# Buffers, a shared key transpose, crossbar-free memory tiles and a reordered start-up in a hybrid encoder layer on one core

## The chip, the cores and the metric

The kernel runs on one core of a Trainium2 chip. A core has a matrix engine (TensorE, PE in the profile; its weight loads are the rows PEld), a vector engine (VectorE, DVE), an activation engine (ScalarE, ACT), GpSimd (POOL) and SyncE (SP), which in this kernel issues every DMA; the rows SPq are its queue. The metric is the device time of one execution in microseconds; less is better. The kernel before takes 3039.52 us, the median of three runs (3033.03 to 3044.13).

## The reference

One encoder layer is applied to two sequences of 4096 and 1024 rows of width 1024 with shared weights. In short:

```python
h = rms_norm(x, norm_in)
z = h @ w_in                          # (L, 1024) @ (1024, 3584)
z_hy, z_att, z_mq, gate = split(z)    # 1152 | 1152 | 256 | 1024 columns
# Hyena branch: centred 3-tap convolution per channel, then an FFT-length convolution
x0, x1, v = split(short_conv3(z_hy));  s = x1 * v
y_hy = x0 * (irfft(rfft(s, 2L) * rfft(filter(L), 2L))[:L] + s * skip)
# 6 heads of 64, three strided windows (128,1) (512,4) (2048,16), merged by their softmax denominators
q, k = head_rms(q), head_rms(k)
y_att = merge(softmax(q k^T / 8 + bias[rel * dil] within |rel| <= R) v  for each window)
# 4 heads of 64 over 256 memory rows
y_mem = softmax(head_rms(z_mq) km^T / 8) vm
out = x + (concat(y_hy, y_att, y_mem) * silu(gate)) @ w_out
```

The filter of the Hyena branch is a small sine network over the positions times an exponential decay per channel.

## The kernel before

**Precision.** The large products are made of three 16-bit matmuls: a value is split into a high and a low fp16 part, and PE adds hi*hi, hi*lo and lo*hi in PSUM (`mm3`, lines 279 to 281). One product of a 128-column weight block with 512 rows is 8 x 3 = 24 matmuls. PSUM has eight banks, given out by tags: "d" has two, "e" two, "f" three and "g" one.

**Stages.** The trace shows five. (1) Start-up: rows of the first block of x are loaded and normed, the first Hyena weight blocks are loaded (`ws`), scaled by the norm gain on POOL (L248), measured on DVE and split by ACT and DVE (L260, L262) into `wh`. (2) `hyena_proj`: ten blocks of 512 rows by nine 128-channel products, tile `zh`; ACT copies each product from PSUM to `zb` (L877), and ACT and DVE apply the three taps (L887, L891). Between them runs the filter stream: `f` (L710), its decay `kt` (L715), a first transform `a` (L732) whose result goes to `fav` (L736, L737). (3) `qkv` products (`z`) woven with the long convolution. (4) Attention woven with the gate products (`zg`). (5) The output product (`oo`).

**One attention tile.** 128 queries of one window, or of the memory. Scores `s` are made by PE from `kT` and `qT`, and from `qS` for half of the heads (L1044, L1047; for the memory L1039). DVE adds the bias and takes the maximum (L1051), negates it (`nm`, L1061), and ACT exponentiates (L1063). The probabilities `pt` must then be transposed and split into fp16 halves. For the first XT = 2 heads of each tile POOL splits them (`hl`, L1079 and L1080) and a transposing DMA, the crossbar, turns them into `hx` (L1082). For the other heads PE transposes in fp32 (`tt`, L1094, four 128x128 blocks for a pair of heads), ACT makes the high half `th` (L1098) and DVE the low half `tl` (L1099). PE multiplies by v (`yp`, L1118 to L1120), ACT, POOL and DVE write the result to `y` (L1155, L1156), and SP stores it to DRAM (`yc`, or `ym` for memory tiles).

**Loads of a group.** Two tiles that share 256 queries form a group; a group's loads are written two groups ahead (AHEAD). `load_group` (L926) asks for three things: the keys `kT` by a transposing DMA of up to 384 rows (L945), the queries `qT` (L946; L933 for memory groups), and `v`. Then DVE makes `qS` (L969), `qT` with the two halves of its partitions exchanged, since a matmul takes both operands from the same partitions.

**What sets the order.** Each stream is a Python generator that yields the cost of what it has just written; `weave` takes the next step from the stream with the least cost so far:

```python
    while live:
        s = min(live, key=lambda v: v[1])
        tc.cur_priority = s[2]
        try:
            s[1] += next(s[0])
```

PE keeps that written order (`manual_schedule` on PE). On every other engine, SP among them, the framework's scheduler orders the instructions by a simulated time line and the priorities; at run time each engine executes its list in order and waits where an operand or a buffer isn't ready. K_A scales the cost of the attention stream against the gates.

Of the kernel before, what the change touches and what calls it, by code (L numbers as in the profile page):

```python
# [22 lines left out]
P = 128  # L23
# [116 lines left out]
K_A, IDLE_A, GATE_IDLE = 0.88, 20000, 0  # L140
LAG_I, WS_BUFS = 6, 6
MT, BATCH0 = 4, 2
MIX, K_Q = 0.1, 1.2
AHEAD = 2
# [34 lines left out]
class Layer:  # L179
# [105 lines left out]
    def setup(self):  # L285
# [9 lines left out]
        self.cinv = {}  # L295
        for i, (off, L) in enumerate(self.seqs):
# [18 lines left out]
    def setup_late(self):  # L315
        nc, c, x = self.nc, self.const, self.x
        self.g_mem = c.tile([P, KC], F32, name="g_mem")
        self.ld(self.g_mem, x["mem_norm"][0].rearrange("(k p) -> p k", p=P))
        self.S_v = c.tile([P, H], F32, name="S_v")
        self.S_mem = c.tile([P, 4], F32, name="S_mem")  # L320
        gains = c.tile([P, 4, E], F32, name="gains")
# [4 lines left out]
        a = c.tile([P, 2, 4], F32, name="gsc")  # L326
# [13 lines left out]
        self.dft = c.tile([P, 4, P], F16, name="dft")  # L340
        self.ld(self.dft, x["dft"].rearrange("p (a b) -> p a b", a=4))
        for i in range(len(self.seqs)):
            self.cinv[i] = c.tile([P, 2, 64], F16, name=f"cinv{i}")
            self.ld(self.cinv[i], x[f"cinv{i}"].rearrange("p (a b) -> p a b", a=2))
# [158 lines left out]
    def memory_weights(self, pool, wpool):  # L503
        nc, x = self.nc, self.x
        self.wm = wm = pool.tile([P, KC, 2, 512], F16, name="wm", bufs=1)
        S = self.S_mem
        for j in (0, 2):
            self.wsplit(
                wpool, self.wparts(x["w_mem_kv"][0], [(j + d, (j + d) * P) for d in range(2)], wm), S[:, j:j + 2],
                self.g_mem, tag="wms", bufs=2,  # L510
            )
# [56 lines left out]
    def bias_tables(self, pool, ps):  # L568
        nc, x, c = self.nc, self.x, self.const
        oh = pool.tile([32, 3, 3 * P], F32, name="oh", bufs=1)  # L570
# [55 lines left out]
    def filter_time(self, pool, psf, small, w1, w2, w3s, delta, m):  # L626
        nc, x = self.nc, self.x
        hid, dec, step, ksum = {}, {}, {}, {}
        for i, (off, L) in enumerate(self.seqs):
# [3 lines left out]
            dec[i] = pool.tile([P, DH], F32, name=f"dec{i}", bufs=1)  # L633
# [70 lines left out]
        def taps(n):  # L704
# [11 lines left out]
            nc.gpsimd.tensor_tensor(out=dec[i], in0=dec[i], in1=step[i], op=ALU.mult)  # L716
# [114 lines left out]
    def hyena_proj(self, pool, ps):  # L831
# [18 lines left out]
        wh, cw, cb = self.hy  # L850
        self.tc.cur_priority += 1500000
        for n, (i, b) in enumerate(blocks):
# [11 lines left out]
            for c in range(3):  # L864
                us = []
                for g in range(3):
# [3 lines left out]
                    z = ps.tile([P, 512], F32, tag="d", name="zh", bufs=2)  # L870
# [35 lines left out]
    def att_tiles(self):  # L906

        out = []
        for i, (off, L) in enumerate(self.seqs):
            for cf, (win, dil) in enumerate(CONFIGS):  # L910
# [6 lines left out]
                for r in range(dil):  # L917
                    for q0 in range(0, n, 256):
                        q1 = min(n, q0 + 256)
                        out.append(dict(  # L920
# [69 lines left out]
    def attention(self, pool, ps):  # L990
# [8 lines left out]
        for g in groups[1:AHEAD]:  # L999
            self.load_group(pool, g)  # L1000
# [682 lines left out]
```

## Time and profile before

| | before |
|---|---|
| median of three runs | 3039.52 us (3033.03 to 3044.13) |
| the profiled execution | 3053.22 us, span 3051.3 us |
| PE busy | 2787.6 us (91%) |
| DVE, ACT, POOL busy | 2054.2, 1663.9, 1263.1 us |
| main DMA queue (SP) | 761578 packets, 75.5% of 16 engines' span |

Busy times are unions of the intervals in which an engine executes. A row of a "waits" view names the instruction that stood first in its engine's list, the instruction whose end released it, the idle time in total, how often, and the longest. A time line's row gives in square brackets the idle time just before it. A "chain" row gives start, length and the link of the chain of work that ended last. In the windows, PEclk is the granted clock of TensorE as a share of its full 2.4 GHz: 0.5 is the lower level of 1.2 GHz. For a DMA row of SPq the duration is that of issuing, not of the transfer.

### The profile page before, as it was taken

The numbers are of one execution on the slowest core, as the hardware profiler recorded it, in microseconds if no ns is written. First come the engines' busy times: TensorE is split into PE (matmuls) and PEld (weight loads), VectorE is DVE, ScalarE is ACT, GpSimd is POOL, SyncE is SP. The second block draws the span as 40 slices with busy tenths as digits, with TensorE's granted clock in tenths as the row PEclk, the third lists the DMA queues.
The fourth block names the chain that finished last, engine by engine and source line by source line (L and its number), as shares of the span: only waits on it lengthen the run. The fifth ranks groups of instructions, "written<-read, shape, count | busy, mean of one in ns | idle before, by whom it ended". The sixth has DMA issues, their size and how long they took to land.

```text
span 3051.3 us, 55381 instructions
## 1 busy us (share of the span) xinstructions
PE 2787.6 (91%) x19620; PEld 1730.6 (57%) x19620; DVE 2054.2 (67%) x5237; ACT 1663.9 (55%) x3149; POOL 1263.1 (41%) x1534
## 2 busy tenths in 40 slices
PE   5898888888899998989999988989899899999999
PEld 2344444334455545544466666666666665778787
DVE  7777888779758872464477666767676666665663
ACT  5666666434668875474266555656566564233321
POOL 3336777343126651151133233333344344555551
PEclk9999999999999999999999999999999999999999
DMA  8555444565579969778499988999998979777762
GB/s 223 176 135 162 133 145 150 170 182 180 195 228 249 249 189 216 220 185 189 134 214 242 218 206 177 219 217 185 209 221 195 206 169 316 247 240 253 236 225 97
DMA packets 761855, 610.38 MB, mean 200 GB/s; under 512 B 514958, under 2 KB 702262, under 8 KB 758122
## 3 DMA queue, kind: packets, MB, share of 16 engines
q1 hardware_dynamic: 761578, 606.84, 75.5%
q8 instruction: 155, 2.54, 0.4%
q14 instruction: 122, 1.00, 0.1%
HBM read 289.08 MB, written 199.92 MB: 160 GB/s over the span
## 4 chain that ended last, share of the span: by engine, by line
PE 37%; DVE 16%; DMA 16%; ACT 7%; issue 6%; POOL 4%; SPq 2%; DVEq 0%; ACTq 0%; POOLq 0%
DMA qT<-rows 5%; PE zg L279 3%; PE zg L280 3%; PE z L279 3%; PE z L280 3%; PE zg L281 3%; PE z L281 3%; PE tt L1094 3%; PE oo L281 2%; PE oo L279 2%; PE oo L280 2%; PE s L1044 2%; DMA gg<-gt 1%; DVE qS L969 1%; PE s L1047 1%
## 5 line engine op out<-in xcount | busy, mean ns | idle before, releaser
L1063 ACT ACTIVATE pt<-pt,nm 128x256 f32<-128x256 f32 (+2 forms) x880 | 350.0, 472 | 187.6 <-DVE nm L1061 178.3
L279 PE MATMUL z<-wA,hA 128*128 128x512 f16 (+1 forms) x960 | 353.9, 369 | 19.8 <-ACT rw L440 11.2
L280 PE MATMUL z<-wA,hA 128*128 128x512 f16 (+1 forms) x960 | 353.2, 368 | 0.0
L281 PE MATMUL z<-wA,hA 128*128 128x512 f16 (+1 forms) x960 | 353.0, 368 | 0.0
L1051 DVE CUSTOM_DVE_ANT_0 pt<-s,tab,lsc 128x256 f32<-128x256 f32 (+1 forms) x672 | 278.6, 449 | 98.6 <-PE s L1047 91.2
L279 PE MATMUL zh<-hB,wh 128*128 128x512 f16 x720 | 280.6, 390 | 27.1 <-ACT zb L877 26.8
L280 PE MATMUL zh<-hB,wh 128*128 128x512 f16 x720 | 280.2, 389 | 1.5 <-DVE hB L384 1.5
L281 PE MATMUL zh<-hB,wh 128*128 128x512 f16 x720 | 279.9, 389 | 0.0
L279 PE MATMUL oo<-wo,mhi 128*128 128x512 f32 x640 | 258.5, 404 | 7.1 <-ACT mhi L1537 3.9
L281 PE MATMUL oo<-wo,mlo 128*128 128x512 f32 x640 | 254.8, 398 | 1.6 <-POOL mlo L1538 1.6
L280 PE MATMUL oo<-wo,mhi 128*128 128x512 f32 x640 | 254.6, 398 | 0.0
L1079 POOL CAST hl<-pt 128x256 f16<-128x256 f32 (+1 forms) x212 | 102.8, 499 | 356.5 <-ACT pt L1063 274.3
L279 PE MATMUL zg<-hG,wg 128*128 128x512 f16 x640 | 247.7, 387 | 0.6 <-DVE vr L475 0.5
L281 PE MATMUL zg<-hG,wg 128*128 128x512 f16 x640 | 247.2, 386 | 0.0
L280 PE MATMUL zg<-hG,wg 128*128 128x512 f16 x640 | 247.2, 386 | 0.0
L1099 DVE TENSOR_TENSOR tl<-tt,th 128x512 f16<-128x512 f32 (+1 forms) x280 | 187.8, 673 | 64.6 <-ACT th L1098 62.7
L1098 ACT ACTIVATE th<-tt 128x512 f16<-128x512 f32 (+1 forms) x280 | 159.3, 574 | 107.6 <-PE yp L1120 54.5
L1094 PE MATMUL tt<-ident,pt 128*128 128x128 f32 x1088 | 172.8, 281 | 40.7 <-DVE tl L1099 29.3
L1044 PE MATMUL s<-kT,qT 128*128 128x256 f16 (+2 forms) x720 | 167.4, 263 | 41.6 <-DVE mx L1051 36.4
L1080 POOL TENSOR_TENSOR hl<-pt,hl 128x256 f16<-128x256 f32 (+1 forms) x212 | 192.0, 913 | 6.4
L891 DVE SCALAR_TENSOR_TENSOR u<-zb,cw,u 128x512 f32<-128x512 f32 (+2 forms) x180 | 163.9, 914 | 36.0 <-ACT u L887 32.7
L1094 PEld LDWEIGHTS tt<-ident,pt 128*128 128x128 f32 x1088 | 131.2, 144 | 76.3 <-issue 36.7
(303 smaller groups left out, 7194.1 us busy)
## 6 DMA issues: line engine op xcount, KB each, us to landing
y<-yc SPq DMA_DIRECT2D x120, 198.0 KB, 4.7
yc<-y SPq DMA_DIRECT2D x112, 198.0 KB, 3.2
xt<-in_x SPq DMA_DIRECT2D x40, 512.0 KB, 4.7
hts<-hB SPq DMA_DIRECT2D x10, 2048.0 KB, 6.5
hA<-hts SPq DMA_DIRECT2D x40, 512.0 KB, 6.3
rows<-rw SPq DMA_DIRECT2D x40, 512.0 KB, 4.1
hG<-hts SPq DMA_DIRECT2D x10, 2048.0 KB
gt<-go SPq DMA_DIRECT2D x80, 256.0 KB, 3.3
```

The costliest lines, as they stand in the source:

```text
L279: nc.tensor.matmul(out, pick_l(lh, k), pick_r(rh, k), start=(k == 0), stop=False)
L280: nc.tensor.matmul(out, pick_l(lh, k), pick_r(rl, k), start=False, stop=False)
L281: nc.tensor.matmul(out, pick_l(ll, k), pick_r(rh, k), start=False, stop=(k == n - 1))
L891: nc.vector.scalar_tensor_tensor(out=u[:, :w], in0=zb[:, c0 + d:c1 + d], scalar=cw[:, j, tap:tap + 1], in1=u[:, :w], op0=ALU.mult, op1=ALU ...
L1044: nc.tensor.matmul(s[:, a, :W], g["qT"][:, h, qs], g["kT"][:, h, kc:kc + W], start=True, stop=False,)
L1051: nc.vector.tensor_tensor_reduce(out=pt[:, h, :W], in0=s[:, a, :W], in1=zero.to_broadcast([P, NMEM]) if mem else tb[:, h, t0:t0 + W], scal ...
L1063: nc.scalar.activation(out=pt[:, h, :W], in_=pt[:, h, :W], func=AF.Exp, bias=nm[:, h:h + 1])
L1079: nc.gpsimd.tensor_copy(hl[:, 0, :, c], src)
L1080: nc.gpsimd.tensor_tensor(out=hl[:, 1, :, c], in0=src, in1=hl[:, 0, :, c], op=ALU.subtract)
L1094: nc.tensor.transpose(tt[:, a, ci, :], pt[:, 2 * pr + a, w0:w0 + P], self.ident)
L1098: nc.scalar.activation(out=th[:, :, :n], in_=tt[:, :, :n], func=AF.Copy)
L1099: nc.vector.tensor_tensor(out=tl[:, :, :n], in0=tt[:, :, :n], in1=th[:, :, :n], op=ALU.subtract)
```

## The change

The diff has these parts:

1. `hyena_proj`: the PSUM tile of `zh` rotates over tags "d", "g", "d", so three banks instead of two; "g" has no other user in that stage.
2. Start-up: BATCH0 2 to 4 puts the first block's four row tiles into one norm chain; WS_BUFS 6 to 3 leaves three buffers for raw Hyena weights; of `setup_late`, the load of the transform `dft` stays there, the gains `gk`, `lsc` move into `bias_tables`, the load of `g_mem` into `memory_weights`, that of `cinv` into `long_conv`.
3. Filter: the decay `dec` gets a second buffer, and its last update is left out.
4. Keys: one `kT` transpose of up to 640 rows serves two groups (KG = 512), with three buffers as before; the `qT` transpose is issued first.
5. `qS`: its two copies move from `load_group` to `swap_queries`, which is written at the last tile of the group before.
6. Memory tiles: XT = 0 for them, so all their heads are transposed on PE.
7. Buffers in attention: `th` and `tl` 4 to 6, `y` 2 to 3; the bias tables are loaded one by one into two buffers.
8. K_A 0.88 to 0.84.

```diff
--- before.py
+++ after.py
...
-K_A, IDLE_A, GATE_IDLE = 0.88, 20000, 0
-LAG_I, WS_BUFS = 6, 6
-MT, BATCH0 = 4, 2
+K_A, IDLE_A, GATE_IDLE = 0.84, 20000, 0
+LAG_I, WS_BUFS = 6, 3
+MT, BATCH0 = 4, 4
 MIX, K_Q = 0.1, 1.2
-AHEAD = 2
+AHEAD, KG = 2, 512
...
-    def setup_late(self):
+    def setup_transforms(self):
+        self.dft = self.const.tile([P, 4, P], F16, name="dft")
+        self.ld(self.dft, self.x["dft"].rearrange("p (a b) -> p a b", a=4))
+
+    def setup_gains(self, pool):
+
         nc, c, x = self.nc, self.const, self.x
-        self.g_mem = c.tile([P, KC], F32, name="g_mem")
-        self.ld(self.g_mem, x["mem_norm"][0].rearrange("(k p) -> p k", p=P))
-        self.S_v = c.tile([P, H], F32, name="S_v")
-        self.S_mem = c.tile([P, 4], F32, name="S_mem")
-        gains = c.tile([P, 4, E], F32, name="gains")
+        gains = pool.tile([P, 4, E], F32, name="gains")
         for i, nm in enumerate(("att_q_norm", "att_k_norm", "mem_q_norm", "mem_k_norm")):
             self.ld(gains[:, i], x[nm][0].partition_broadcast(P))
         self.gk = c.tile([P, 2, E], F32, name="gk")
         nc.vector.tensor_tensor(out=self.gk, in0=gains[:, 0:4:2], in1=gains[:, 1:4:2], op=ALU.mult)
-        a = c.tile([P, 2, 4], F32, name="gsc")
+        a = pool.tile([P, 2, 4], F32, name="gsc")
...
-        self.dft = c.tile([P, 4, P], F16, name="dft")
-        self.ld(self.dft, x["dft"].rearrange("p (a b) -> p a b", a=4))
-        for i in range(len(self.seqs)):
-            self.cinv[i] = c.tile([P, 2, 64], F16, name=f"cinv{i}")
-            self.ld(self.cinv[i], x[f"cinv{i}"].rearrange("p (a b) -> p a b", a=2))
...
+        self.setup_gains(pool)
...
-            dec[i] = pool.tile([P, DH], F32, name=f"dec{i}", bufs=1)
+            dec[i] = pool.tile([P, DH], F32, tag=f"dec{min(i, 1)}", name="dec", bufs=2 - min(i, 1))
...
-            nc.gpsimd.tensor_tensor(out=dec[i], in0=dec[i], in1=step[i], op=ALU.mult)
+            d = dec[i]
+            if n2 + 1 < 2 * self.seqs[i][1] // N1:
+                dec[i] = pool.tile([P, DH], F32, tag="dec0", name="dec", bufs=2)
+                nc.gpsimd.tensor_tensor(out=dec[i], in0=d, in1=step[i], op=ALU.mult)
...
+                    nz += 1
-                    z = ps.tile([P, 512], F32, tag="d", name="zh", bufs=2)
+                    z = ps.tile([P, 512], F32, tag="dgd"[nz % 3], name="zh", bufs=2 - nz % 3 % 2)
...
-                    for q0 in range(0, n, 256):
-                        q1 = min(n, q0 + 256)
-                        out.append(dict(
-                            seq=i, cf=cf, dil=dil, r=r, n=n, pair=False, q0=q0, nq=q1 - q0,
-                            k0=max(0, q0 - 64), k1=min(n, q1 + 64),
-                        ))
+                    for b0 in range(0, n, KG):
+                        b1 = min(n, b0 + KG)
+                        keys = dict(b0=b0, k0=max(0, b0 - 64), k1=min(n, b1 + 64))
+                        for q0 in range(b0, b1, 256):
+                            q1 = min(n, q0 + 256)
+                            out.append(dict(
+                                seq=i, cf=cf, dil=dil, r=r, n=n, pair=False, q0=q0, nq=q1 - q0, keys=keys,
+                                k0=max(0, q0 - 64), k1=min(n, q1 + 64),
+                            ))
...
-        kT = pool.tile([P, 6, 384], F16, tag="kT", name="kT", bufs=AHEAD + 1)
-        nk = g["k1"] - g["k0"]
+        if g["cf"] not in self.tab:
+            self.load_table(pool, g["cf"])
+        if g["pair"] or g["q0"] == g["keys"]["b0"]:
+            kT = pool.tile([P, 6, KG + P], F16, tag="kT", name="kT", bufs=3)
...
-            nc.sync.dma_start_transpose(out=kT[:, :, :nk], in_=rows[r, g["k0"]:g["k1"], C_K:ROW])
             nc.sync.dma_start_transpose(
                 out=qT[:, :, :g["nq"]], in_=rows[r, g["q0"]:g["q0"] + g["nq"], C_Q:C_MQ]
             )
+            keys = g["keys"]
+            if g["q0"] == keys["b0"]:
+                keys["kT"] = kT
+                nc.sync.dma_start_transpose(
+                    out=kT[:, :, :keys["k1"] - keys["k0"]], in_=rows[r, keys["k0"]:keys["k1"], C_K:ROW]
+                )
+            kT = keys["kT"]
             cuts = [g["k0"]] + list(range(g["q0"] + 64, g["k1"], 128))
...
+    def swap_queries(self, pool, g):
+
+        if "mem" in g:
+            return
+        nc, qT = self.nc, g["qT"]
         qS = g["qS"] = pool.tile([P, 6, 256], F16, tag="qS", name="qS", bufs=2)
         for a in range(2):
             nc.vector.tensor_copy(
@@ -994,10 +1017,10 @@
...
-        self.load_group(pool, groups[0])
-        self.load_tables(pool)
-        for g in groups[1:AHEAD]:
+        self.tab = {}
+        for g in groups[:AHEAD]:
             self.load_group(pool, g)
+        self.swap_queries(pool, groups[0])
         yield IDLE_A
...
+            if (t + 1) * P == g["nq"] and gi + 1 < len(groups):
+                self.swap_queries(pool, groups[gi + 1])
...
-                st["chunks"] = [(0, 0), (P, 1)]
+                st["chunks"], st["xt"] = [(0, 0), (P, 1)], 0
...
+                st["xt"] = XT
...
-                if h + 1 == XT:
+                if h + 1 == st["xt"]:
                     crossbar(st)
...
-            for pr in range(XT // 2, st["H"] // 2):
+            for pr in range(st["xt"] // 2, st["H"] // 2):
...
-                th = pool.tile([P, 2, 2, P], F16, tag="th", name="th", bufs=4)
-                tl = pool.tile([P, 2, 2, P], F16, tag="tl", name="tl", bufs=4)
+                th = pool.tile([P, 2, 2, P], F16, tag="th", name="th", bufs=6)
+                tl = pool.tile([P, 2, 2, P], F16, tag="tl", name="tl", bufs=6)
...
-            heads = list(range(XT, st["H"])) + list(range(XT))
-            st["p"] += [(st["hx"][:, 0, h], st["hx"][:, 1, h]) for h in range(XT)]
+            heads = list(range(st["xt"], st["H"])) + list(range(st["xt"]))
+            st["p"] += [(st["hx"][:, 0, h], st["hx"][:, 1, h]) for h in range(st["xt"])]
...
-        y = pool.tile([P, YW], F32, tag="y", name="y", bufs=2)
+        y = pool.tile([P, YW], F32, tag="y", name="y", bufs=3)
...
+        self.cinv[i] = self.const.tile([P, 2, 64], F16, name=f"cinv{i}")
+        self.ld(self.cinv[i], x[f"cinv{i}"].rearrange("p (a b) -> p a b", a=2))
...
+    def load_table(self, pool, cf):
+        nc = self.nc
+        t = self.tab[cf] = pool.tile([P, H, 256], F32, tag="tab", name="tab", bufs=2)
+        src = self.tab_d[cf]
+        self.ld(t, bass.AP(src.tensor, src.offset + P - 1, [[H * 384 - 1, P], [384, H], [1, 256]]))
+        if cf == len(CONFIGS) - 1:
+            bm = pool.tile([P, P], F32, tag="y", name="bm", bufs=3)
+            self.ld(bm, self.x["bmask"])
+            self.tabp = pool.tile([P, H, P], F32, name="tabp", bufs=1)
+            nc.gpsimd.tensor_tensor(
+                out=self.tabp, in0=t[:, :, 64:192], in1=bm.unsqueeze(1).to_broadcast([P, H, P]), op=ALU.add
+            )
```

**Attention, DVE.** These rows of the list of DVE stand at a memory tile in the middle of attention. `pt,mx` are the bias and maximum, `nm` its negation, `tl` the low half of the transposed probabilities, `qS` the exchanged queries of the next group. Before:

```order
L1051 ISA pt,mx<-s,zero,lsc 128x256
L1051 ISA mx 128x1
L1051 ISA pt,mx<-s,zero,lsc 128x256
L1051 ISA mx 128x1
L1061 TENSOR_SCALAR nm<-mx 128x4
L969 COPY qS<-qT 64x6x128 x2
L1099 TENSOR_TENSOR tl<-tt,th 128x512
L1051 ISA pt,mx<-s,zero,lsc 128x256
L1051 ISA mx 128x1
```

In the changed kernel, at a memory tile of the same part of the program:

```order
L1077 ISA pt,mx<-s,zero,lsc 128x256
L1077 ISA mx 128x1
L1077 ISA pt,mx<-s,zero,lsc 128x256
L1077 ISA mx 128x1
L1125 TENSOR_TENSOR tl<-tt,th 128x512
L1077 ISA pt,mx<-s,zero,lsc 128x256
L1077 ISA mx 128x1
L1077 ISA pt,mx<-s,zero,lsc 128x256
L1077 ISA mx 128x1
L992 COPY qS<-qT 64x6x128 x2
L1125 TENSOR_TENSOR tl<-tt,th 128x512
```

The two copies of `qS` stand in the middle of a tile's work in both lists, behind scores of that tile and ahead of a `tl`; `tl` appears more often, since memory tiles now make two.

**Attention, SP.** These rows are of the queue that issues all DMAs; `rows_75` and `rows_77` are the same DRAM tensor of q and k of the long sequence (`rows_105`, `rows_107` of the short one), `yc` the stores of results, `gt` of gates. Before:

```order
L946 DMA_TRANSPOSE qT<-rows_75 128x6x256
L195 DMA yc_1_84<-y 128x396
L945 DMA_TRANSPOSE kT<-rows_75 128x6x384
L1082 DMA_TRANSPOSE hx<-hl 128x8x128
L192 DMA v<-vrows_106 128x774
L195 DMA gt_3_90<-go 128x512
L192 DMA v<-vrows_106 64x774 x2
L1082 DMA_TRANSPOSE hx<-hl 128x8x128
L195 DMA yc_1_84<-y 128x396
L946 DMA_TRANSPOSE qT<-rows_75 128x6x256
L945 DMA_TRANSPOSE kT<-rows_105 128x6x256
```

In the changed kernel:

```order
L956 DMA_TRANSPOSE qT<-rows_77 128x6x256
L195 DMA gt_3_92<-go 128x512
L962 DMA_TRANSPOSE kT<-rows_77 128x6x576
L1108 DMA_TRANSPOSE hx<-hl 128x8x128
L195 DMA yc_1_86<-y 128x396
L192 DMA v<-vrows_78 128x2x774
L192 DMA v<-vrows_78 64x774
L195 DMA yc_1_86<-y 128x396
L956 DMA_TRANSPOSE qT<-rows_107 128x6x256
```

`kT` of 384 rows became one of 576 that stands behind `qT`, and the second `qT<-rows_107` has no `kT` of its own; between the loads stand fewer `hx`.

**Start-up, ACT.** `xn,nv<-xt` squares a row tile for its norm, `rs_y` makes the inverse root, `xn<-xt,rs_y` scales, `hB` is the transposed block, `wh` the high half of a weight block, `zb` the first product's copy. Before:

```order
L359 ACTIVATE xn,nv<-xt 128x1024
L365 ACTIVATE xn<-xt,rs_y 128x1024 x2
L359 ACTIVATE xn,nv<-xt 128x1024
L386 ACTIVATE hB<-xt_242 128x1024
L386 ACTIVATE hB<-xt_264 128x1024
L359 ACTIVATE xn,nv<-xt 128x1024
L260 ACTIVATE wh<-ws,wsa 128x8x128 x2
L359 ACTIVATE xn,nv<-xt 128x1024
L260 ACTIVATE wh<-ws,wsa 128x8x128 x3
L877 ACTIVATE zb<-zh 128x512
```

In the changed kernel:

```order
L260 ACTIVATE wh<-ws,wsa 128x8x128 x2
L357 ACTIVATE xn,nv<-xt 128x1024
L203 ACTIVATE rs_y<-rs_t 128x4
L363 ACTIVATE xn<-xt,rs_y 128x1024 x4
L883 ACTIVATE zb<-zh 128x512
L893 ACTIVATE u<-zb,cb,cw 128x511
L883 ACTIVATE zb<-zh 128x512
L893 ACTIVATE u<-zb,cb,cw 128x511
L883 ACTIVATE zb<-zh 128x512
L893 ACTIVATE u<-zb,cb,cw 128x511
L357 ACTIVATE xn,nv<-xt 128x1024
L260 ACTIVATE wh<-ws,wsa 128x8x128 x3
```

Four squares, one `rs_y` and four scales stand in a row now, where two rounds of two stood; the three weight blocks behind the first two (`wh` x3) moved from ahead of the first `zb` to behind the third.

## Rows read from the trace of the kernel before

**Rows 1.** Windows: us, busy per engine, PEclk, DMA share, GB/s.

```profile
38.00:712.00 674.00, 604.86 (x2746) 277.36 (x2746) 531.26 (x942) 383.23 (x629) 350.47 (x426) 0.96 0.53 158
...
1521.00:2515.00 994.00, 903.54 (x9929) 641.60 (x9928) 683.65 (x2490) 608.06 (x1385) 361.64 (x606) 0.97 0.95 206
```

**Rows 2.** Waits of PE, whole run: total us, times, longest.

```profile
PE s L1044 <- DVE mx L1051: 36.4, 25, 4.4
PE tt L1094 <- DVE tl L1099: 29.3, 20, 4.9
PE zh L279 <- ACT zb L877: 26.8, 10, 4.4
...
PE f L710 <- DVE kt L715: 18.7, 19, 3.6
```

**Rows 3.** Time line of PE: the first zh, and two rows 24 matmuls apart.

```profile
38.03 0.58 PE L279 MATMUL zh<-hB,wh 128*128 128x512 f16 x1 [0.26 <-ACT hB L386]
...
44.06 0.38 PE L281 MATMUL zh<-hB,wh 128*128 128x512 f16 x1
...
49.24 0.38 PE L281 MATMUL zh<-hB,wh 128*128 128x512 f16 x1
```

**Rows 4.** Windows in the Hyena stage, after one zb wait.

```profile
122.00:129.00 7.00, 5.60 (x12) 2.04 (x12) 7.00 (x9) 4.54 (x7) 3.88 (x4) 0.52 0.75 253
```

**Rows 5.** Waits of ACT, 560 to 712 us.

```profile
ACT wA L260 <- DVE wsa L257: 21.0, 3, 11.3
```

**Rows 6.** Time line of SP, start-up: start, length of issuing.

```profile
17.70 1.56 SPq L192 DMA_DIRECT2D g_mem<-in_mem_norm  x1
...
24.45 12.27 SPq L192 DMA_DIRECT2D xt<-in_x  x4
...
42.37 2.15 SPq L192 DMA_DIRECT2D ws<-in_w_in  x2
```

**Rows 7.** Time line of ACT, start-up.

```profile
30.93 1.06 ACT L359 ACTIVATE xn<-xt 128x1024 f32<-128x1024 f32 x1 [6.25 <-DMA xt<-in_x]
...
71.41 3.21 ACT L260 ACTIVATE wh<-ws,wsa 128x1024 f16<-128x1024 f32 x3
```

**Rows 8.** Time line of POOL, start-up.

```profile
50.92 3.75 POOL L248 TENSOR_TENSOR ws<-ws,g_in 128x1024 f32<-128x1024 f32 x2 [2.69 <-DMA ws<-in_w_in]
```

**Rows 9.** Waits of DVE in attention.

```profile
DVE qS L969 <- DMA qT<-rows: 87.7, 38, 5.9
```

**Rows 10.** Waits of POOL in attention.

```profile
POOL y L1155 <- DMA yc<-y: 153.9, 54, 6.2
```

**Rows 11.** Chain of waits around one qS wait: start, us, what.

```profile
2247.03 0.44 PE tt L1094 x4
...
2253.57 5.14 DMA qT<-rows
...
2259.87 0.55 DVE qS L969
...
2262.83 0.43 PE zg L279
...
2266.03 0.22 PE zg L280
```

**Rows 12.** Time line of PE at the same wait.

```profile
2262.08 0.75 PE L1094 MATMUL tt<-ident,pt 128*128 128x128 f32 x4 [4.86 <-DVE tl L1099]
```

**Rows 13.** Groups by shape in attention: busy us, mean ns, idle before.

```profile
L1099 DVE TENSOR_TENSOR tl<-tt,th 128x512 f16<-128x512 f32 x264 | 181.1, 688 | 61.0 <-ACT th L1098 59.2 <-PE yp L1120 0.3
...
L1098 ACT ACTIVATE th<-tt 128x512 f16<-128x512 f32 x264 | 153.4, 586 | 101.0 <-PE yp L1120 48.9 <-PE tt L1094 36.4 <-PE yp L1119 15.1
...
L1094 PE MATMUL tt<-ident,pt 128*128 128x128 f32 x1088 | 172.8, 281 | 40.7 <-DVE tl L1099 29.3 <-DVE nm L1061 7.7 <-DVE sm L1148 2.3
```

**Rows 14.** Tile kT: issuing on SP, ns min/median/max.

```profile
L945 SPq DMA_TRANSPOSE kT<-rows x56: 1347/2354/9177, 1503.6 to 2476.4; - x56
```

**Rows 15.** Tile hx: issuing on SP, ns min/median/max.

```profile
L1082 SPq DMA_TRANSPOSE hx<-hl x160: 1190/1287/5897, 1538.5 to 2509.5; - x160
```

More of the change, by code (lines that the diff above doesn't have):

```diff
@@ L295, in setup @@
         self.cinv = {}
+        self.S_v = c.tile([P, H], F32, name="S_v")
+        self.S_mem = c.tile([P, 4], F32, name="S_mem")
         for i, (off, L) in enumerate(self.seqs):
@@ L504, in memory_weights @@
         nc, x = self.nc, self.x
+        g_mem = pool.tile([P, KC], F32, name="g_mem")
+        self.ld(g_mem, x["mem_norm"][0].rearrange("(k p) -> p k", p=P))
         self.wm = wm = pool.tile([P, KC, 2, 512], F16, name="wm", bufs=1)
@@ L509, in memory_weights @@
                 wpool, self.wparts(x["w_mem_kv"][0], [(j + d, (j + d) * P) for d in range(2)], wm), S[:, j:j + 2],
-                self.g_mem, tag="wms", bufs=2,
+                g_mem, tag="wms", bufs=2,
             )
@@ L850, in hyena_proj @@
         wh, cw, cb = self.hy
+        nz = 0
         self.tc.cur_priority += 1500000
@@ L1026, in scores @@
                     st["chunks"] = [(0, g["chunks"][ks]), (ke - ks - P, g["chunks"][q0 + 64])]
-                W, kc = ke - ks, ks - g["k0"]
+                W, kc = ke - ks, ks - (g["k0"] if g["pair"] else g["keys"]["k0"])
+                st["xt"] = XT
                 st["v"], st["lo"] = g["v"], VH
@@ L1563, in output @@
             self.st(self.out[i][t0:t0 + P, :], xr)
-    def load_tables(self, pool):
+    def load_table(self, pool, cf):
         nc = self.nc
-        self.tab = []
-        for cf in range(3):
-            t = pool.tile([P, H, 256], F32, name=f"tab{cf}", bufs=1)
-            src = self.tab_d[cf]
-            self.ld(t, bass.AP(src.tensor, src.offset + P - 1, [[H * 384 - 1, P], [384, H], [1, 256]]))
-            self.tab.append(t)
-        bm = pool.tile([P, P], F32, tag="pt", name="bm", bufs=3)
-        self.ld(bm, self.x["bmask"])
-        self.tabp = pool.tile([P, H, P], F32, name="tabp", bufs=1)
-        nc.gpsimd.tensor_tensor(
-            out=self.tabp, in0=self.tab[2][:, :, 64:192], in1=bm.unsqueeze(1).to_broadcast([P, H, P]), op=ALU.add
-        )
+        t = self.tab[cf] = pool.tile([P, H, 256], F32, tag="tab", name="tab", bufs=2)
[8 more added lines that the diff above has]
+            )
     def pool(self, name, space=None, side=None):
@@ L1602, in filters @@
                     yield IDLE_F
-                    self.setup_late()
+                    self.setup_transforms()
                     yield from scaled(sub(lambda p: self.hyena_filter(p, ps), "right"), K_F)
```

## The prediction

> **What bounds the kernel now.** I read the table of busy times first, then the windows by stage, the waits of PE, the time lines of start-up, and last the waits of DVE in attention with the chain around one of them. PE is busy 91% of the span, so what can be gained is its idle time, the stretches at the lower clock, and work taken off it; what is put on it costs in full. Of the Hyena stage's 674 us PE lacks 69, of attention's 994 it lacks 90.5 [rows 1]. In the Hyena stage three causes are named: the copy `zb` that frees a bank of `zh` (26.8 us, ten times, longest 4.4), the decay product `kt` (18.7 us), and the buffer `fav`, which the change leaves alone [rows 2]. In attention PE is released mostly by DVE, through `mx` and `tl` [rows 2]. But DVE is busy only 684 of 994 us there [rows 1]; it is late because it stands idle for 87.7 us, 38 times, at the copy `qS`, until the transposed queries land [rows 9]. One case shows the whole path: the DMA of `qT` takes 5.14 us, `qS` follows, and then the `tl` behind it [rows 11]; PE has stood 4.86 us at the transposes that wait for that `tl` [rows 12]. So the stage is bound by PE with breaks whose origin lies in the queue of SP, not by a busy DVE.
>
> **Hyena stage, a third bank.** A product is 24 matmuls: 49.24 - 44.06 = 5.18 us at the full clock [rows 3]. With a third bank PE may run one product further ahead of the copy, which is longer than the longest of the ten waits, 4.4 us [rows 2]; so all ten should go, -26.8 us. After four of them the clock falls to the lower level of 1.2 GHz for some 7 us; in the window of one PE is busy 5.60 us at a granted 0.52, work for 2.9 us at the full clock, so 2.7 us are lost, 10.8 for four [rows 4]. The upper end is thus -38. Not all of it stays: the last three waits fall after 632 us, where ACT waits 21.0 us for the weights of the next stage [rows 5], and a PE that is early there waits for those weights instead. I take -25, ends -38 and -10.
>
> **Hyena stage, the decay.** With two buffers POOL no longer waits for `kt` before it updates `dec`, and `kt` no longer for an update made late. At most the 18.7 us at `f` [rows 2] go; but each `kt` still needs the update before it and its turn on DVE, which is busy 79% of this stage [rows 1]. I take -6, ends 0 and -18.7.
>
> **Start-up.** Taken off SP ahead of the second four row tiles are `g_mem` and four `gains` (from 17.70; their requests and those of `dft` and `cinv`, which stay, fill the time to 24.45) [rows 6]. ACT waits 6.25 us for these rows [rows 7], yet the requests themselves then take 12.27 us to be issued [rows 6], so the transfers are at their limit; the norm chain in one piece saves a round on DVE and ACT. I put the first `zh` about 6 us ahead of 38.03 [rows 3]. Against this stand the weights. With six buffers the blocks for the second three products were requested long before; with three they wait until ACT and DVE have split earlier ones. From the request at 42.37 to the end of the scaling on POOL it took 50.92 + 3.75 - 42.37 = 12.3 us [rows 6, 8], and the split of three takes 3.21 on ACT [rows 7], with measuring on DVE between: some 20 us from request to use. Buffers come free at about 36, so those weights are ready at about 57, where PE, three products after its first and with the slow matmuls of its first five us [rows 3], wants them at about 49: 8 us of waiting, and some 3 more at the last three blocks. Sum +5, ends -6 and +15.
>
> The constants moved behind the filter, and `cinv`, cost nothing on PE: few small loads, in stretches where the queues are used half (DMA share 0.53) [rows 1]. If that cover fails, it is the 4.8 us that they take on SP, once.
>
> **Attention, the wait for the queries.** By the case above 4.86 of at most 5.9 us reach PE [rows 9, 12], so about 0.82 x 87.7 = 72 us of PE's 90.5 idle ones hang on it. After that case the steps of `zg` take 0.43 us instead of 0.22 from 2262.83 to 2266.03: 3.2 us at the lower clock, 1.6 lost [rows 11]. What does the change do to it? Writing the copies later (`swap_queries`) does little by itself: the order of DVE shows the two copies in the middle of a tile's work in both kernels, since the scheduler had placed them there, by a time line in which the queries land earlier than they do. What helps is SP: 40 fewer `hx` requests at 1.287 us are 51 us [rows 15], 18 fewer `kT` at 2.354 are 42, of which the longer ones give some back [rows 14]; together 80 to 93 of 994 us, and the crossbar moves fewer small packets while the DMA engines are busy 95% [rows 1]. `qT` no longer stands behind its own `kT`, and a third `y` shortens the waits of the stores that stand ahead of `qT`; POOL's 153.9 us behind those stores [rows 10] aren't on PE's path. But the request must come some 5 us earlier to clear a wait, and a lighter queue gives that only where it was late by its own load. I take 40% of 72, -28, with -6 of clock; ends 0 and -72 (and -14 of clock).
>
> **Attention, buffers and work.** Six `th` and `tl` can only help the part of the 29.3 us at `tt` [rows 2] that isn't the same wait: -6, ends 0 and -12. In each of 40 memory tiles one more pair of heads is transposed on PE, four blocks: 160 transposes, 40 `th` and 40 `tl`. Four take 0.44 us in the chain [rows 11]: 160 x 0.11 = 17.6 us, on PE in full; by the group's busy time, 172.8/1088, it is 25.4 [rows 13]. I take +18. DVE gets 40 x 0.688 = 27.5 us, ACT 40 x 0.586 = 23.4 [rows 13]; beside a third of DVE's time idle I count +5, ends 0 and +27. K_A only moves some gate products behind the last tile, where PE does them just the same: 0.
>
> The Trainium skill (TensorE: Matmul & The Clock Gate, Part 4: PE-mode transpose) speaks against this edit: in a kernel measured there the full clock did not engage for PE's transposes. Here four transposes run in 0.44 us with full-speed `zg` on both sides, which doesn't bear it out for bursts of four; its consequence is the third rival.
>
> **Sum.** Hyena stage -25 - 6 + 5 = -26; attention -28 - 6 - 6 + 18 + 5 = -17; the conv/qkv and output stages unchanged. -43 on the profiled execution's 3053.2 is 3010; that execution lies 13.7 above the median of 3039.5, so the median becomes about 2996; I say 2995.
>
> **Rivals.**
> *The queries' wait goes altogether.* The copy, written a group's last tile later, would never be ahead of the landing: attention -72 - 14 - 6 + 18 + 5 = -69, total -95, 2945. For it: every one of the 38 waits ends with the same DMA [rows 9]. Against it: the unchanged place in the order of DVE.
> *The wait stays as it is.* SP's relief is used up by its own waits for `hl` and `y`, and the copies stay too early. Then attention is -6 + 18 + 5 = +17, total -9, 3030. For it: the same order, and a landing time of 5 us that no edit shortens by itself.
> *Slower: the added transposes break the clock.* If each of 40 added bursts brought a drop like the one in the chain, at 1.6 us [rows 11], that is +64 on the forecast's -43: 3060. It decides from 27 of the 40 bursts on. Against it: 1088 transposes, 272 bursts, stand in the stage already; with 3.2 us at half speed behind each, its granted clock would be near 0.56 and it is 0.97 [rows 1, 13]. For it: memory tiles will make bursts closer together than any tile now does.
>
> **How the numbers follow.** The forecast has 0.50, with its own range 2970 to 3020; the first rival 0.20, the second 0.17, the third 0.13. A change of 0.3%, 9 us, is about what can be told from none. The forecast and the first rival are faster, the second lies at the border and gives 0.05 to faster and 0.12 to same, the third is slower: 0.75, 0.12, 0.13. The range 2945 to 3045 leaves out the third rival and part of the first.
>
> **What would show it.** In the new profile: no wait of `zh` on `zb`, and fewer stretches at the lower clock before 700; a first `zh` near 32 and a wait of PE for `wh` near 50 to 57; DVE's wait at `qS` for `qT` near 50 us instead of 87.7, if it is below 15 the first rival holds, above 75 the second; 1248 `tt`. Wrong would I be if attention doesn't get shorter than 994 us by about 17, or if its granted clock falls below 0.95.

## The result, and the profile after

The changed kernel takes 3010.78 us, the median of four runs (3008.71 to 3015.35), against 3037.43 for the kernel before on the same chip (the three runs above and a fourth): a ratio of 0.9912 with a 95% interval of 0.989 to 0.9935, 26.7 us less. Its profiled execution took 3008.71 us, the one of before 3053.22; that one lies some 16 us above its own median, so the two traces differ by 44.5 us, more than the runs do. What follows is read from the traces.

How far two traces of the same code differ can be read from this case as well. The stretch from the first `z` to the first `s`, which no experiment edits, takes 812 to 822 us over all its traces, and attention, where its code is the same, 957.2, 968.1 and 959.5 us (the changed kernel, and the experiments with six weight buffers and with two banks). So a difference of some 10 us in such a stage between two single traces is not yet an effect.

| from the traces, us | before | after | difference so far |
|---|---|---|---|
| first `zh` | 38.0 | 31.5 | -6.5 |
| first `zh` of the second block | 90.7 | 109.4 | +18.7 |
| last `zh` of the second block | 157.1 | 164.7 | +7.6 |
| last `zh` | 701.3 | 688.1 | -13.2 |
| first `z` | 701.5 | 696.4 | -5.1 |
| first `s` of attention | 1521.2 | 1511.7 | -9.5 |
| end of the last `yp` fed by a `th` | 2514.7 | 2468.9 | -45.8 |
| end | 3051.3 | 3006.9 | -44.4 |

So nearly all of the gain came in attention, 993.5 us before (first `s` to that `yp`) and 957.2 after, 25 to 36 us by the three traces just named, and the Hyena stage gave almost nothing. First the two windows of after, from the first `zh` to the end of the first block and attention (length, busy time per engine, PEclk, DMA share, GB/s; attention answers to [rows 1]):

```profile
31.50:110.80 79.30, 51.78 (x223) 22.24 (x223) 59.16 (x111) 35.71 (x48) 24.33 (x27) 0.83 0.65 194
1511.70:2468.90 957.20, 897.53 (x10064) 650.46 (x10062) 688.36 (x2528) 629.48 (x1424) 286.93 (x526) 0.98 0.86 199
```

PE lacks 27.5 of the first 79 us. In attention it lacks 59.7 us, where it lacked 90.5. The waits of PE after, in the order of the list (total us, times, longest; to be held against [rows 2]):

```profile
PE zh L279 <- ACT wh L260: 27.5, 2, 16.7
PE s L1070 <- DVE mx L1077: 25.2, 28, 5.4
...
PE tt L1120 <- DVE tl L1125: 16.7, 14, 3.3
PE f L711 <- DVE kt L716: 13.5, 15, 2.3
...
PE z L279 <- ACT zb L883: 7.9, 1, 7.9
...
PE zh L279 <- ACT zb L883: 4.7, 2, 2.6
```

The wait of `zh` for `zb` fell from 26.8 to 4.7 us, that for `kt` by 5.2. A new one heads the list, 27.5 us for split weights `wh`, in two pieces. Here they are in the time line of PE:

```profile
31.52 0.38 PE L279 MATMUL zh<-hB,wh 128*128 128x512 f16 x1 [0.83 <-ACT hB L384]
58.05 0.61 PE L279 MATMUL zh<-hB,wh 128*128 128x512 f16 x1 [10.83 <-ACT wh L260]
92.14 0.61 PE L279 MATMUL zh<-hB,wh 128*128 128x512 f16 x1 [16.67 <-ACT wh L260]
```

The matmuls behind both waits take 0.61 us where the first took 0.38: the clock is at its lower level there, after PE had stood still. The path of the last three weight blocks, by the time lines of SP, POOL, DVE and ACT:

```profile
59.52 6.14 SPq L192 DMA_DIRECT2D ws<-in_w_in  x3
```

```profile
67.83 7.60 POOL L248 TENSOR_TENSOR ws<-ws,g_in 128x1024 f32<-128x1024 f32 x3 [0.71 <-DMA ws<-in_w_in]
```

```profile
84.69 4.65 DVE L225 COPY peaks<-peak 32x32 f32<-32x32 f32 x4
```

```profile
90.94 3.23 ACT L260 ACTIVATE wh<-ws,wsa 128x1024 f16<-128x1024 f32 x3 [13.94 <-DVE wsa L257]
```

From the request at 59.5, when the three buffers had come free, to the split at 90.9 it took 31.4 us; 15.5 of them pass between the end of the scaling on POOL at 75.4 and the split, while DVE measures the blocks between steps of the next block's norm. In attention the surprise is the row of DVE that answers to [rows 9]:

```profile
DVE qS L992 <- DMA qT<-rows: 87.4, 37, 6.1
```

DVE waits for the queries as long as before, 87.4 against 87.7 us, and PE stands still a third less. One such wait in the time line of DVE:

```profile
1783.25 1.12 DVE L992 COPY qS<-qT 64x1536 f16<-64x1536 f16 x2 [3.49 <-DMA qT<-rows]
```

DVE stands from 1779.76 to 1783.25, and PE runs through, with transposes and gate products:

```profile
1780.25 0.38 PE L281 MATMUL zg<-hG,wg 128*128 128x512 f16 x1
...
1781.91 0.60 PE L1120 MATMUL tt<-ident,pt 128*128 128x128 f32 x4
...
1783.00 0.38 PE L280 MATMUL zg<-hG,wg 128*128 128x512 f16 x1
```

What lets it run through stands in the waits of ACT in attention. Before:

```profile
ACT th L1098 <- PE yp L1120: 54.5, 41, 5.4
ACT th L1098 <- PE tt L1094: 37.2, 37, 2.3
ACT th L1098 <- PE yp L1119: 15.1, 11, 2.3
```

After:

```profile
ACT th L1124 <- PE tt L1120: 100.6, 108, 4.3
```

Before, ACT waited 69.6 us, 52 times, for PE to finish a `yp` and so free one of the four buffers; the `tl` behind it and the next `tt` then came late as well. With six, `th` waits only for its input. Its idle time in all is hardly less, 106.8 us before and 100.6 after, but ACT now stands because it is early, and no longer holds up `tl` and `tt`. The code sets a tile's `yp` two tiles behind its `tt` at the least, and each tile of a window makes two pairs: four buffers are just what is in flight, and leave nothing for a stall.

### The profile page after: what moved, and what is told of

The parts are those of the page before. It is cut to its first block, busy times and chain, and to the rows that moved or that the text cites. A ratio compares the mean times of both kernels' runs of the same rounds, so it can differ in the third digit from the quotient of the medians.

```text
span 3006.9 us, 55527 instructions
## 1 busy us (share of the span) xinstructions
PE 2774.9 (92%) x19780; PEld 1737.1 (58%) x19780; DVE 2067.4 (69%) x5272; ACT 1684.7 (56%) x3188; POOL 1188.5 (40%) x1452
## 4 chain that ended last, share of the span: by engine, by line
PE 45%; DVE 13%; DMA 12%; ACT 6%; issue 5%; POOL 2%; SPq 1%; POOLq 0%; ACTq 0%; DVEq 0%
DMA qT<-rows 4%; PE zg L279 4%; PE zg L280 4%; PE zg L281 4%; PE tt L1120 3%; PE z L280 3%; PE z L281 3%; PE z L279 3%; PE oo L279 3%; PE oo L280 3%; PE oo L281 3%; PE s L1070 2%; PE s L1073 2%; ACT kt L1370 1%; DVE pt L1077 1%
## 5 line engine op out<-in xcount | busy, mean ns | idle before, releaser
L279 PE MATMUL zh<-hB,wh 128*128 128x512 f16 x720 | 278.9, 387 | 33.1 <-ACT wh L260 27.5
L1125 DVE TENSOR_TENSOR tl<-tt,th 128x512 f16<-128x512 f32 (+1 forms) x320 | 214.5, 674 | 65.3 <-ACT th L1124 63.3
L279 PE MATMUL zg<-hG,wg 128*128 128x512 f16 x640 | 244.7, 382 | 1.3 <-DVE vr L473 1.3
L281 PE MATMUL zg<-hG,wg 128*128 128x512 f16 x640 | 245.1, 383 | 0.0
L280 PE MATMUL zg<-hG,wg 128*128 128x512 f16 x640 | 244.9, 383 | 0.0
L1124 ACT ACTIVATE th<-tt 128x512 f16<-128x512 f32 (+1 forms) x320 | 182.3, 574 | 101.5 <-PE tt L1120 100.6
L1120 PE MATMUL tt<-ident,pt 128*128 128x128 f32 x1248 | 193.5, 277 | 23.9 <-DVE tl L1125 16.7
L1105 POOL CAST hl<-pt 128x256 f16<-128x256 f32 (+1 forms) x172 | 78.1, 471 | 333.1 <-ACT pt L1089 290.1
L1120 PEld LDWEIGHTS tt<-ident,pt 128*128 128x128 f32 x1248 | 149.2, 143 | 58.5 <-issue 18.2
L1073 PE MATMUL s<-kT,qS 128*128 128x256 f16 (+2 forms) x720 | 165.1, 260 | 0.0
```

Source lines behind the costliest of these rows:

```text
L279: nc.tensor.matmul(out, pick_l(lh, k), pick_r(rh, k), start=(k == 0), stop=False)
L280: nc.tensor.matmul(out, pick_l(lh, k), pick_r(rl, k), start=False, stop=False)
L281: nc.tensor.matmul(out, pick_l(ll, k), pick_r(rh, k), start=False, stop=(k == n - 1))
L1073: nc.tensor.matmul(s[:, a, :W], g["qS"][:, h, qs], g["kT"][:, h, kc:kc + W], start=False, stop=True,)
L1105: nc.gpsimd.tensor_copy(hl[:, 0, :, c], src)
L1120: nc.tensor.transpose(tt[:, a, ci, :], pt[:, 2 * pr + a, w0:w0 + P], self.ident)
```

## The experiments

Times are compared as ratios to the kernel before, run on the same chip; the changed kernel's is 0.9912 (0.989 to 0.9935).

**Six weight buffers.**

```diff
-LAG_I, WS_BUFS = 6, 3
+LAG_I, WS_BUFS = 6, 6
```

> The changed kernel with six raw weight buffers instead of three, all else kept. In the changed kernel PE waits 27.5 us for the weights wh at start-up, in two waits (10.8 near 58 us, 16.7 near 92). Theory A, the three buffers cost that: the waits fall to under 5 us in sum, the first block's products end some 20 us earlier, and the last zh comes near 668 instead of 688. Theory A1: the gain stays, the first z follows at once, time about 17 us less than the changed kernel, ratio to before about 0.985. Theory A2: the next stage's weights are ready no earlier, the first z stays near 690 to 696 and its wait grows from 8 to 20 us or more; ratio about 0.991, as the changed kernel. Rival: the weights are late by DVE's and ACT's order and not by the buffers, so the two waits stay above 20 us.

Ratio 0.9848 (0.9817 to 0.9879). The wait for `wh` is gone from the list of PE; the first block ends at 82.6 us instead of 109.4, the last `zh` at 673.0 and the first `z` comes at 679.6, 16.8 us earlier than in the changed kernel. The last `zh` was expected near 668. Theory A holds, and A1: the next stage's weights came earlier with the rest, and the wait at the first `z` is 6.2 us instead of 7.9. The row of ACT shows what that wait is, the last `zb` behind a split of weights, as in the changed kernel:

```profile
675.86 3.23 ACT L260 ACTIVATE wA<-ws,wsa 128x1024 f16<-128x1024 f32 x3 [4.07 <-DVE wsa L257]
678.99 0.57 ACT L883 ACTIVATE zb<-zh 128x512 f32<-128x512 f32 x1
```

**Four `th` and `tl`.**

```diff
-                th = pool.tile([P, 2, 2, P], F16, tag="th", name="th", bufs=6)
-                tl = pool.tile([P, 2, 2, P], F16, tag="tl", name="tl", bufs=6)
+                th = pool.tile([P, 2, 2, P], F16, tag="th", name="th", bufs=4)
+                tl = pool.tile([P, 2, 2, P], F16, tag="tl", name="tl", bufs=4)
```

> The changed kernel with four th and tl buffers instead of six. In attention (first s to last yp) the changed kernel takes 957 us against 994, though DVE's wait at qS is the same (87.4 and 87.7 us); of PE's idle time 48 us instead of 70 stand within 4 us of such a wait. Theory B: the two more buffers let PE run on through a stall of DVE; then without them attention is 15 to 25 us longer, PE waits for tl rise from 16.7 to about 28, ratio to before about 0.998. Rival C (another part did it, the memory tiles or the place of the copies): attention stays within 5 us of 957, ratio about 0.991.

Ratio 0.9987 (0.9971 to 1.0003): without this part the whole change is worth nothing that can be told. The third `y`, K_A and the bias tables, which no run takes out one by one, are in that rest. Attention takes 993.5 us, PE waits 46.6 us for `tl`, and ACT waits for `yp` again, for 159 us:

```profile
PE tt L1120 <- DVE tl L1125: 46.6, 30, 9.0
...
ACT th L1124 <- PE yp L1146: 93.7, 86, 4.4
ACT th L1124 <- PE yp L1145: 65.4, 36, 12.1
```

Theory B holds, within its 15 to 25 us: by the ratios the two buffers are worth 0.0075, or 23 us. The traces' 36 us rest on the shortest of the three traces of attention, and are 25 against the longest.

**Memory tiles on the crossbar again.**

```diff
-                st["chunks"], st["xt"] = [(0, 0), (P, 1)], 0
+                st["chunks"], st["xt"] = [(0, 0), (P, 1)], XT
```

> The changed kernel with the memory tiles back on the crossbar for two of their heads: 1088 tt instead of 1248, 160 hx instead of 120. Theory C: the crossbar's transfers made PE's idle time, so without that part attention is longer by 10 to 20 us in spite of 18 us less of PE's transposes; ratio about 0.996. Rival D: the 160 transposes are a plain cost; attention is 12 to 20 us shorter, ratio about 0.986. If both weigh the same, within 5 us of the changed kernel.

Ratio 0.9923 (0.9899 to 0.9947), as the changed kernel. PE's busy time in attention falls by 23.7 us (897.5 to 873.8), its idle time rises by 18.9 (59.7 to 78.6), and DVE's wait at `qS` is 106.0:

```profile
1520.40:2472.80 952.40, 873.82 (x9838) 629.48 (x9836) 674.74 (x2489) 607.09 (x1381) 360.35 (x606) 0.97 0.95 211
```

The third outcome: the transposes cost about what was reckoned, and the time can't tell the two ways apart.

**The copies written behind the loads again.**

```diff
-    def swap_queries(self, pool, g):
...
-            if (t + 1) * P == g["nq"] and gi + 1 < len(groups):
-                self.swap_queries(pool, groups[gi + 1])
```

> The changed kernel with the copies qS written in load_group again, right behind the loads. Theory E: the scheduler places the copies by its own time line and the place in the code matters little: DVE's wait at qS stays between 75 and 100 us, time within 6 us of the changed kernel, ratio 0.989 to 0.993. Rival F: the later place is what took 22 us off PE's idle time; then attention is 15 to 25 us longer, ratio about 0.998, and the wait at qS rises above 100 us.

Ratio 0.99 (0.9865 to 0.9934), wait at `qS` 92.6 us: theory E, the place in the code does nothing that can be told.

**Six `th` and `tl` in the kernel before, alone.** The edit of the second experiment the other way round, in the kernel before.

> The kernel before with one part of the change alone: six th and six tl buffers instead of four. Theory B1: with four buffers a stall of DVE at qS comes through to PE, whatever the tiles are; then this part alone takes attention from 993 us to about 955 to 970 (no added transposes), ratio 0.987 to 0.992. Rival B2: four buffers are short only with the memory tiles' second pair, so that the six only pay for that; then attention stays within 8 us of 993, ratio 0.997 to 1.002, and the changed kernel's gain needs both parts.

Ratio 0.9921 (0.9899 to 0.9943): this part alone gives what the whole change gives. Attention takes 973.7 us, 3.7 above the band of B1 and far from B2's; `th` has no wait for `yp` left, and PE waits 12.6 us for `tl` instead of [rows 2]'s 29.3:

```profile
ACT th L1098 <- PE tt L1094: 74.6, 80, 3.5
...
PE tt L1094 <- DVE tl L1099: 12.6, 7, 5.4
```

By the ratios the buffers are worth 24 us alone and 23 on top of the rest of the change, and the rest without them 0.0013: the parts add up to the whole, and it takes no second pair of the memory tiles to make four buffers short.

**The copies on POOL.**

```diff
-            nc.vector.tensor_copy(
+            nc.gpsimd.tensor_copy(
                 qS[64 * a:64 * a + 64, :, :g["nq"]], qT[64 - 64 * a:P - 64 * a, :, :g["nq"]]
```

> The changed kernel with six weight buffers, and the two copies qS on POOL instead of DVE. DVE then has no wait for qT (98 us before) and 55 to 70 us less work. Theory G: the wait at qS is what still breaks PE in attention; PE's idle time there falls from about 60 to 20 us, attention from 957 to 968 to about 915 to 930, ratio 0.970 to 0.976. Rival H: POOL's copies come late behind its own waits for stores (147 us at y), so that PE waits for qS itself; attention stays or gets longer, ratio 0.985 to 1.00, with waits of s on qS in the list of PE.

Ratio 1.0054 (1.0027 to 1.008), the only one above 1. DVE has no wait for `qT`, and attention takes 1041.5 us. Theory G fails, and H in its detail too: PE doesn't wait for `qS`. It waits for the crossbar's tiles, since POOL now stands for the queries with `hl` queued behind. The head of PE's waits, and POOL's:

```profile
PE yp L1144 <- DMA hx<-hl: 58.9, 15, 7.2
PE s L1070 <- DVE mx L1077: 37.6, 34, 5.3
```

```profile
POOL qS L992 <- DMA qT<-rows: 67.9, 27, 8.6
```

The wait had only changed engines, so its cause lay ahead of the copy.

**One `kT` per group, and then ten `th` and `tl`.** Both with six weight buffers.

```diff
-AHEAD, KG = 2, 512
+AHEAD, KG = 2, 256
```

> The changed kernel with six weight buffers, and one kT transpose per group as before (KG 256): 18 more kT requests. Theory I: the lighter queue of SP counts, attention 5 to 15 us longer than with KG 512, ratio about 0.988. Rival J: DVE's wait at qS didn't shrink with the lighter queue, so the key transposes are off the path; attention within 5 us of 968, ratio 0.983 to 0.987.

> As the run before it (KG 256 frees the room), with ten th and ten tl buffers instead of six. Theory B: more buffers let PE run on through longer stalls; waits of tt for tl fall from 17 to under 8 us, attention another 8 to 15 us shorter, ratio about 0.981. Rival K: six already cover what they can, since the two PSUM banks of tt and the three of s hold PE as soon as DVE stands still; within 4 us.

Ratios 0.9833 (0.9808 to 0.9858) and 0.9826 (0.9799 to 0.9853), waits at `qS` 88.8 and 86.3, attention 963.8 and 959.9. The shared transpose gives nothing (J), and buffers beyond six give nothing that can be told (K): the waits for `tl` are 17.7 and 15.5.

**A fourth buffer for the queries.** On the kernel with KG 256 and six weight buffers:

```diff
-        qT = g["qT"] = pool.tile([P, 6, 256], F16, tag="qT", name="qT", bufs=AHEAD + 1)
+        qT = g["qT"] = pool.tile([P, 6, 256], F16, tag="qT", name="qT", bufs=AHEAD + 2)
```

> The changed kernel with six weight buffers, KG 256 and a fourth buffer for qT; nothing else. With three, SP's request for the queries waits for a buffer that the group two before still reads. Theory L: that buffer is why the copies qS always stand close behind the request; with a fourth the request goes out a group's work earlier, DVE's wait at qS falls from 95 to under 30 us, PE's idle time in attention from 60 to about 25, attention from 964 to about 925, ratio about 0.971. Rival M: the earlier requests only move the delay, since the DMA engines are busy 86% there and kT, v or hx come later in their place; DVE's wait falls, but PE waits for v, hx or kT, attention within 10 us of 964, ratio 0.980 to 0.986.

Ratio 0.97 (0.9668 to 0.9732), 2955.45 us: the fastest of all, ahead of both kernels. Attention with the fourth buffer, and then DVE's wait there without it (KG 256, six weight buffers) and with it:

```profile
1496.20:2414.10 917.90, 888.40 (x10064) 646.25 (x10063) 694.48 (x2528) 629.91 (x1424) 289.00 (x526) 0.99 0.94 213
```

```profile
DVE qS L992 <- DMA qT<-rows: 88.8, 37, 8.0
...
DVE qS L992 <- DMA qT<-rows: 32.5, 12, 5.0
```

Theory L: PE's idle time falls to 29.5 us, as was expected to within 5, and DVE's wait ends a little above the 30 that were expected; the waits of PE for `hx` and `v` are 0.7 and 3.0. In the trace each group's last request for `qT` on SP was paired in order with its first copy on DVE. The copy starts a median 5.3 us behind the request in the kernel before and in the changed kernel, about as long as the transfer takes (a median 4.6 us to landing in the kernel before); with the fourth buffer it is 11.7, and 17 of 64 copies start within 7 us instead of 48 and 40.

**All loads a group earlier** (AHEAD 3, four buffers for `kT`).

> As the run before it, with all loads of a group asked for one group earlier (AHEAD 3, four buffers for kT and qT, two for v as before). Theory L: as the fourth qT buffer alone, within 8 us of it. Rival N: asked for earlier, the v loads stand in SP's queue waiting for their two buffers, and hold up the crossbar transfers behind them: attention longer than with the fourth buffer alone by 10 us or more, with waits of PE on hx or v.

Ratio 0.9702 (0.9665 to 0.974), the same. Attention is 10.6 us longer with 11.9 us of waits for `v`, as rival N said, but the total doesn't tell the two apart:

```profile
PE yp L1144 <- DMA v<-vrows: 11.9, 4, 5.3
```

**Two banks for `zh`**, with six weight buffers.

```diff
-                    z = ps.tile([P, 512], F32, tag="dgd"[nz % 3], name="zh", bufs=2 - nz % 3 % 2)
+                    z = ps.tile([P, 512], F32, tag="d", name="zh", bufs=2)
```

> The changed kernel with six weight buffers and two banks for zh as before. With three banks the Hyena products run from 31.8 to 672.6 us (640.8), in the kernel before from 38.0 to 700.9 (662.9). Theory O: the bank is worth most of that: the waits of zh for zb come back to about 25 us, the products take 20 to 30 us longer, the first z comes near 697 and waits little, ratio about 0.992. Rival P: the decay's second buffer and the rest did it, then the products stay within 8 us of 641.

Ratio 0.9862 (0.9832 to 0.9892), not to be told from 0.9848. The waits for `zb` are back, the products take 651.4 us instead of 641.2, but the first `z` comes at 685.2 and waits 1.1 us: 5.6 later than with three banks. Between O and P; part of the bank's gain is handed back at the next stage's weights.

```profile
PE zh L279 <- ACT zb L883: 23.9, 13, 6.5
```

**The fourth query buffer in the kernel before, alone.**

> The kernel before with a fourth buffer for qT and nothing else (so four th and tl, the crossbar for memory tiles, copies written behind the loads, kT ahead of qT). Theory L: the queries' landing is what breaks PE in attention there too; DVE's wait at qS falls from 88 to 25 to 45 us, attention from 993 to about 945, ratio 0.982 to 0.988. Rival Q: with four th and tl the rest of the stalls still comes through, and SP's heavier queue takes the lead back: attention above 975, ratio above 0.992.

Ratio 0.9909 (0.9885 to 0.9933): this one line also gives what the whole change gives. DVE's wait falls only to 56.3 us and the ratio is above the band of theory L, but attention is 953.4 us, near its 945. ACT's waits of `th` for `yp` stay at 64.7 us, so the two repairs are different ones.

```profile
DVE qS L969 <- DMA qT<-rows: 56.3, 21, 5.4
...
ACT th L1098 <- PE yp L1120: 43.8, 38, 3.9
...
ACT th L1098 <- PE yp L1119: 20.9, 16, 2.2
```

## Why the prediction was right, and where it wasn't

The time, 3010.8, lies within the range; the forecast of 2995 asked for 42 to 44 us less and 27 were measured, so the sum of -43 was some 16 too large. In the traces, which differ by 44.4 us, it looks as if it were met. But the traced execution of before lies 16 above its median and that of the changed kernel 2 below its own, so that much of the difference is no gain, and the traces can't tell in which stage it sits. That the time still lies in the range is in part luck, since the terms were each off: the Hyena stage was to give 26 and gave 5, attention 17 and gave 25 to 36 in the traces. The 28 us of the queries' wait didn't come, and the buffers `th` and `tl`, put at 6, brought 23 in their place.

*Third bank and decay.* Right in kind, too large in size: the ten waits for `zb` shrank to two, `kt` gave 5.2 us for a forecast of 6. From the second block's end to the last `zh` the stage is 20.8 us shorter, where the two terms asked for 31. The bank was put at 25 and is worth some 10 us of the products by the experiment with two banks, though 23.9 us of waits come back there, and 5.6 at the first `z`. Handing back at the next stage's weights was foreseen, and shown by that experiment.

*Start-up.* Here the term was mis-sized. The first `zh` came at 31.5 for "near 32", and the first wait was 10.8 us at 58 where 8 at 57 were forecast. The second, "some 3 more", was 16.7 us. The 20 us from request to use were put together from the kernel before, where the last blocks were scaled long ahead; with three buffers request, scaling and measuring stand in a row beside the next block's norms, 31.4 us. The sum was +5, inside its own band of -6 to +15, and the measured +18.7 at the first block's end is outside it; 7.6 are left at the second block's end. Six buffers show that it is the buffers, and bring the first `z` 16.8 us forward.

*The queries' wait.* This step failed. SP's lighter queue was to bring 28 us; the wait stayed at 87.4 us, and was 88.8 without the shared `kT`. By the prediction's own sign, above 75, the mechanism of the second rival held. It isn't that the queue got no relief. The prediction priced the requests by their medians, but a few long ones weigh more: summed over the trace, the issues of `kT` took 162.8 us before and 116.8 after, those of `hx` 252.1 and 187.1, together 111 us less for 80 to 93 forecast (the issues of `qT` took 7 more). The relief of the queue didn't reach the wait.

```profile
L962 SPq DMA_TRANSPOSE kT<-rows x38: 1397/3264/6178, 1497.1 to 2428.1; - x38
```

The request is late by its landing buffer: by the code, with three, it can go only when the group before the present one is through. The fourth buffer cuts the wait in both kernels, which shows this half. That the scheduler puts the copy just behind the landing that it reckons with is argued from the lists and from the place in the code making no difference, and was not tested by itself. The 6 and 14 us of clock beside this term were stated without a working; the granted clock of attention rose from 0.97 to 0.98.

*`th` and `tl`.* Mis-sized: forecast -6, with ends 0 and -12; measured by the ratios 24 us alone and 23 on top of the rest. I took the 29.3 us of PE's waits for `tl` for the queries' wait and left it there. Both had a share: a stall of DVE costs PE only what the buffers behind it can't bridge. ACT's wait for `yp`, 69.6 us, would have told it; it stood in the row of `th` in [rows 13], as 48.9 and 15.1 us for the full tiles, and was not read.

*The transposes.* The busy time of `tt` rose from [rows 13]'s 172.8 to 193.5 us, 20.7 for a forecast of 18. The granted clock of attention is 0.98 against 0.97, so the third rival fell. That less waiting could pay for the part had been left out.

*Swap.* Right: it does nothing that can be told. The first rival's 38 waits were not touched, and the second rival, "the wait stays", was true of the wait and not of its price.

## What to carry to other kernels

When an engine in the middle of a chain waits for the end of the chain to give a buffer back, the buffers just cover what is in flight, and a stall anywhere can go through: look for such rows on the engines that aren't the bound. When a wait ends with a transfer, ask what the request itself waited for, an issue slot or a buffer to land in; another landing buffer was worth more here than any relief of the queue. Fewer buffers for raw data show at the one place where the pipeline fills.

## What the runs showed of the hardware

The same copy of 64 x 1536 fp16 elements took a median 1.46 us on POOL and 0.55 on DVE. The issue of a transposing DMA on SP varied more from one to the next than with its rows: 1.35 to 9.18 us, on average 2.91, for up to 384 rows of `kT`, and 1.40 to 6.18, on average 3.07, for up to 640. After the two stops of 10.8 and 16.7 us at start-up the matmuls ran at the lower clock level, and the window around them has a granted clock of 0.83.
